# Sums for the projections' quads queued behind weight splits, and attention's moving operands read alternately from two places 2 KB apart

## The chip, the cores and the metric

The kernel runs on one core of one Trainium2 chip. Its time is the device time of one launch in microseconds (us). Five engines work side by side, each with its own queue of instructions: TensorE (PE, with the weight loads shown as PEld), VectorE (DVE), ScalarE (ACT), GpSimd (POOL) and SyncE (SP), which here only issues DMAs. An instruction starts when those ahead of it on its engine have gone and the semaphores that it waits for are set.

## The reference

Two layers over an input x of 256 rows by 2048 columns, all in float32. Layer A projects the normed input to q, k, v and a gate (4096 columns each), does attention in chunks of 64 rows with a bias per relative distance for 32 heads of 128, multiplies by SiLU of the gate and projects back to 2048 columns. Layer B does the same with a shared k and v, a forget gate and a causal mask. Cut to what matters:

```python
h = rms_norm(x, a_norm[layer])                        # layer A
q, k, v, g = jnp.split(h @ a_w_in[layer], 4, axis=-1)
o = chunked_relbias_attention(q, k, v, a_rel_bias[layer])
x = x + (o * jax.nn.silu(g)) @ a_w_out[layer]

h_kv = rms_norm(x, kv_norm)                           # layer B
k_sh, v_sh = jnp.split(h_kv @ kv_w, 2, axis=-1)
cum = cumsum(log_sigmoid(h_kv @ f_w + f_b))
q, g = jnp.split(rms_norm(x, b_norm[0]) @ b_w_in[0], 2, axis=-1)
o = forgetting_attention(q, k_sh, v_sh, cum)
x = x + (o * jax.nn.silu(g)) @ b_w_out[0]
return rms_norm(x, final_norm)
```

## The kernel before, in words

**Products in three parts.** Each float32 operand is split into a high part (rounded to the type fp32r, written by ACT) and a low part (what is left, by a subtraction on DVE). A product is then three fp32r matmuls: high by high, high by low, low by high. `mm3` (L184) does it for the projections, `dot3` (L517 to L519) for attention and for the quads below.

**The stream of weights.** SP loads blocks of 512 KB (256 rows of the weights by 512 columns) into a ring of six raw buffers. `Feed.prepare` splits a block ("hi" on ACT, "lo" on DVE: L247 and L248, in layer B with a gain L242 and L243) into a ring of four hi and lo buffers, three blocks ahead of the block that PE multiplies. One block is 12 matmuls with 512 moving columns. The block lies in SBUF as [128, 2, 2, 256]; `cols` (L70 to L72) makes the moving operand read its 512 columns alternately from the two halves, which are 2 KB apart.

**Groups.** Two heads make a group, 16 groups a layer. A group of layer A is two units of eight blocks (aqk: q and k; avg: v and gate), one of layer B also (bqg: q and gate; bkv: k and v). While PE multiplies one unit, the attention of an earlier group is woven in by a generator (`attention`) that is advanced between blocks. Its steps for one group: DVE transposes q and k in squares of 32 (L487), POOL's queue moves the squares by 16 DMAs (`turned`), ACT and DVE split k and q into "wide" and "q1" (L509, L510), PE makes the scores (s1p, six matmuls of 256 columns, L517 to L519, and s0p, two float32 ones, L541), DVE scales and adds the bias (L548) and takes the maximum (L549), ACT takes the exponential (L551), ACT scales the gate (L562), DVE transposes the lot (`sgY`, L487), 16 DMAs move it (`sgZ`), ACT and DVE split the probabilities into the same "wide" (L509, L510), PE multiplies by v (op, six matmuls of 256 columns and two float32 ones, L575), and DVE multiplies by the gate (L579). A float32 matmul is four passes on PE in the records.

Each "wide" part is a tile of [128, heads, 256], so the 256 moving columns of one head lie next to each other.

**Quads.** After each layer comes the output projection (ao, bo: four units of 512 columns, 16 blocks each). For some pairs of blocks the kernel uses seven products where the plain way has eight (`Quad`): three such quads for ao0 and ao1, five for each later pair. For this, sums of blocks of the attention's output have to be formed: `Quads.open` (L361 to L380) forms five sets. One set is, on DVE, one addition of 128x512 (L371), four of 128x128 (L374 to L377), a copy by ACT (L378) and a subtraction on DVE (L379). The generator is advanced during the blocks ahead of the first quad. A scheduler then places the instructions of each engine by when their inputs are expected, so DVE's instructions for a set stand earlier in its queue than the code has them. `tc.issue_after(x)` keeps the instructions that are made within it behind the instruction x on x's engine. `feed.by_dve` is the latest split that the stream has put on DVE.

The lines are those of the kernel before; in the changed kernel they are up to 13 higher.

## Time and profile before

| what | value |
|---|---|
| time, median of 3 runs | 1755.29 us (1753.59 to 1757.29) |
| the profiled execution's own time | 1757.04 us |
| its span | 1755.3 us |
| PE busy | 1738.7 us, 99% |
| DVE, ACT, POOL busy | 1243.2, 1107.2, 516.6 us |
| DMA | 396.35 MB, mean 226 GB/s |

The span runs from the first instruction of the profile to the last; the 1.74 us by which the time is longer lie around it. A row of the timeline has the start in us, the duration in us, the engine, the line, the operation, the tiles (out <- in), the shape and a count of merged instructions, and in brackets how long the engine sat idle before it and what ended that. Matmuls are pipelined: the duration of one is longer than its distance to the next, so what a matmul costs is read from start to start. The page says also that ends of matmuls are modelled.

### The profile page before, as it was taken

The numbers are of one execution on the slowest core, as the hardware profiler recorded it, in microseconds if no ns is written. First come the engines' busy times: TensorE is split into PE (matmuls) and PEld (weight loads), VectorE is DVE, ScalarE is ACT, GpSimd is POOL, SyncE is SP. The second block draws the span as 40 slices with busy tenths as digits, with TensorE's granted clock in tenths as the row PEclk, the third lists the DMA queues.
The fourth block names the chain that finished last, engine by engine and source line by source line (L and its number), as shares of the span: only waits on it lengthen the run. The fifth ranks groups of instructions, "written<-read, shape, count | busy, mean of one in ns | idle before, by whom it ended". The sixth has DMA issues, their size and how long they took to land.

```text
span 1755.3 us, 25640 instructions
## 1 busy us (share of the span) xinstructions
PE 1738.7 (99%) x8348; PEld 1527.7 (87%) x8348; DVE 1243.2 (71%) x1818; ACT 1107.2 (63%) x2103; POOL 516.6 (29%) x1071
## 2 busy tenths in 40 slices
PE   9999999999999999999999999999999999999997
PEld 7888888888888888888888888888888888888886
DVE  7666666666666686688966777777777777876687
ACT  6555555555555566556657777777777777665454
POOL 2333333333333333202103333333333333333000
PEclk9999999999999999999999999999999999999999
DMA  8776776776777677677767777777767777767654
GB/s 301 241 222 222 227 225 223 226 224 225 224 222 226 224 224 230 202 241 250 245 214 234 226 226 224 224 227 225 224 226 225 225 226 225 245 214 233 218 203 144
DMA packets 143654, 396.35 MB, mean 226 GB/s; under 512 B 31104, under 2 KB 38560, under 8 KB 143392
## 3 DMA queue, kind: packets, MB, share of 16 engines
q1 hardware_dynamic: 107472, 354.25, 62.9%
q0 software_dynamic: 32256, 37.29, 6.5%
q10 hardware_dynamic: 3792, 3.17, 0.6%
q8 instruction: 66, 1.08, 0.3%
q14 instruction: 68, 0.56, 0.1%
HBM read 351.05 MB, written 4.23 MB: 202 GB/s over the span
## 4 chain that ended last, share of the span: by engine, by line
PE 96%; DMA 1%; DVE 1%; ACT 0%; issue 0%; SPq 0%; POOL 0%; DVEq 0%; ACTq 0%
PE bkv_acc L184 19%; PE bqg_acc L184 19%; PE avg_acc L184 18%; PE aqk_acc L184 18%; PE bo_acc L184 8%; PE ao_acc L184 7%; PE op L575 1%; PE s0p L541 1%; PE p L519 0%; PE p L517 0%; PE p L518 0%; PE op L518 0%; PE s1p L518 0%; PE s1p L519 0%; PE s1p L517 0%; PE op L519 0%
## 5 line engine op out<-in xcount | busy, mean ns | idle before, releaser
L490 POOL DMA_DIRECT2D sgZ<-sgY x512 | 251.0, 497 | 193.8 <-DVE sgY L487 90.6
L490 POOL DMA_DIRECT2D turned<-turned x448 | 219.9, 498 | 265.3 <-PE avg_acc L184 94.7
L243 DVE SCALAR_TENSOR_TENSOR bqg_lo<-bqg_raw,gain,bqg_hi 128x512 fp32r<-128x512 f32 x256 | 182.6, 750 | 84.4 <-ACT bqg_hi L242 84.2
L242 ACT ACTIVATE bqg_hi<-bqg_raw,gain 128x512 fp32r<-128x512 f32 x256 | 170.7, 714 | 107.4 <-PE bqg_acc L184 51.8
L248 DVE TENSOR_TENSOR avg_lo<-avg_raw,avg_hi 128x1024 fp32r<-128x1024 f32 x127 | 153.3, 1219 | 109.6 <-ACT avg_hi L247 107.9
L248 DVE TENSOR_TENSOR aqk_lo<-aqk_raw,aqk_hi 128x1024 fp32r<-128x1024 f32 x125 | 152.4, 1219 | 86.8 <-ACT aqk_hi L247 85.4
L247 ACT ACTIVATE avg_hi<-avg_raw 128x1024 fp32r<-128x1024 f32 x127 | 132.4, 1055 | 121.2 <-PE aqk_acc L184 68.6
L243 DVE SCALAR_TENSOR_TENSOR bkv_lo<-bkv_raw,gain,bkv_hi 128x512 fp32r<-128x512 f32 x256 | 181.0, 748 | 38.3 <-ACT bkv_hi L242 35.6
L184 PE MATMUL bqg_acc<-bqg_hi,x1Th 128*128 128x512 f32 x512 | 192.2, 386 | 0.0
L184 PE MATMUL aqk_acc<-aqk_hi,xTh 128*128 128x512 f32 x512 | 190.4, 382 | 1.5 <-ACT aqk_hi L247 1.5
L184 PE MATMUL aqk_acc<-aqk_lo,xTh 128*128 128x512 f32 x512 | 189.1, 380 | 1.2 <-DVE aqk_lo L248 1.2
L184 PE MATMUL avg_acc<-avg_hi,xTh 128*128 128x512 f32 x512 | 190.2, 382 | 0.0
L184 PE MATMUL bqg_acc<-bqg_lo,x1Th 128*128 128x512 f32 x512 | 189.6, 381 | 0.0
L184 PE MATMUL bqg_acc<-bqg_hi,x1Tl 128*128 128x512 f32 x512 | 189.4, 380 | 0.0
L184 PE MATMUL bkv_acc<-bkv_hi,x1Th 128*128 128x512 f32 x512 | 189.1, 380 | 0.0
L247 ACT ACTIVATE aqk_hi<-aqk_raw 128x1024 fp32r<-128x1024 f32 x125 | 131.5, 1052 | 91.2 <-PE aqk_acc L184 43.5
L184 PE MATMUL bkv_acc<-bkv_lo,x1Th 128*128 128x512 f32 x512 | 188.9, 379 | 0.0
L184 PE MATMUL avg_acc<-avg_lo,xTh 128*128 128x512 f32 x512 | 188.9, 379 | 0.0
L184 PE MATMUL avg_acc<-avg_hi,xTl 128*128 128x512 f32 x512 | 188.9, 379 | 0.0
L184 PE MATMUL bkv_acc<-bkv_hi,x1Tl 128*128 128x512 f32 x512 | 188.9, 379 | 0.0
L184 PE MATMUL aqk_acc<-aqk_hi,xTl 128*128 128x512 f32 x512 | 188.9, 379 | 0.0
L242 ACT ACTIVATE bkv_hi<-bkv_raw,gain 128x512 fp32r<-128x512 f32 x256 | 168.7, 712 | 22.9 <-PE bqg_acc L184 16.5
(297 smaller groups left out, 3556.0 us busy)
## 6 DMA issues: line engine op xcount, KB each, us to landing
bqg_raw<-in_b_w_in SPq DMA_DIRECT2D x128, 512.0 KB, 4.3
bkv_raw<-in_kv_w SPq DMA_DIRECT2D x128, 512.0 KB, 4.0
avg_raw<-in_a_w_in SPq DMA_DIRECT2D x127, 512.0 KB, 4.2
aqk_raw<-in_a_w_in SPq DMA_DIRECT2D x125, 512.0 KB, 3.9
ao_raw<-in_a_w_out SPq DMA_DIRECT2D x64, 512.0 KB, 4.4
bo_raw<-in_b_w_out SPq DMA_DIRECT2D x64, 512.0 KB, 4.1
sgZ<-sgY POOLq DMA_DIRECT2D x512, 40.0 KB, 4.0
turned<-turned POOLq DMA_DIRECT2D x448, 32.0 KB, 3.7
```

The costliest lines, as they stand in the source:

```text
L184: pe.matmul(acc[t], x[:, t * P:(t + 1) * P], w, start=t not in begun, stop=last and i == 2)
L242: act.activation(hi[:, :, j], raw[:, :, j], AF.Copy, scale=gk)
L243: dve.scalar_tensor_tensor(lo[:, :, j], raw[:, :, j], gk, r32(hi[:, :, j]), op0=OP.mult, op1=OP.subtract)
L247: self.by_act = act.activation(hi[:, :, j], raw[:, :, j], AF.Copy)
L248: self.by_dve = dve.tensor_sub(lo[:, :, j], raw[:, :, j], r32(hi[:, :, j]))
L490: queues[j].dma_start(out=r32(z)[j * SQ:(j + 1) * SQ, i], in_=y[i * SQ:(i + 1) * SQ, j])
L541: pe.matmul(s0p[:, i], q0[:, i], qkT[:, HG + i, 0], start=True, stop=True)
L575: pe.matmul(op[:, i, P:], v1[:, i * DH:(i + 1) * DH], pT[:, i, NT], start=False, stop=i == HG - 1)
```

## The change

Two parts. In `Quads.open` the work on a set of sums is put within `tc.issue_after(feed.by_dve.ins)`. In `split_pairs` high and low parts become one tile with the two halves t of a head's 256 columns 2 KB apart ("wide") or, for q1, one half; the moving operand then takes a column of each half in turn. The scores and the outputs come out with their columns interleaved, so DVE reads PSUM with a step of two (two instructions for s1p, one per head, where there was one), the float32 matmul of op writes every second column of PSUM, and the forget gate's matmuls (zp, L799 and L800) and their copy go the same way. The tiles in which the start's input lies are named anew.

```diff
--- before.py
+++ after.py
@@ -368,15 +368,16 @@
                 self.sums.append(two[:, b % 2])
                 hi, lo = two[:, b % 2, 0], two[:, b % 2, 1]
                 k = b * KB
-                dve.tensor_add(xs, r32(lhs.hi[k // BIG][:, k % BIG:k % BIG + KB]),
-                               r32(lhs.lo[k // BIG][:, k % BIG:k % BIG + KB]))
-                a11, a21, a12, a22 = (xs[:, j, t * P:(t + 1) * P] for j in range(KB) for t in range(NT))
-                dve.tensor_add(v[:, 0], a21, a22)
-                dve.tensor_sub(v[:, 2], a11, a21)
-                dve.tensor_sub(v[:, 1], v[:, 0], a11)
-                dve.tensor_sub(v[:, 3], a12, v[:, 1])
-                act.activation(hi, v, AF.Copy)
-                dve.tensor_sub(lo, v, r32(hi))
+                with tc.issue_after(feed.by_dve.ins):
+                    dve.tensor_add(xs, r32(lhs.hi[k // BIG][:, k % BIG:k % BIG + KB]),
+                                   r32(lhs.lo[k // BIG][:, k % BIG:k % BIG + KB]))
+                    a11, a21, a12, a22 = (xs[:, j, t * P:(t + 1) * P] for j in range(KB) for t in range(NT))
+                    dve.tensor_add(v[:, 0], a21, a22)
+                    dve.tensor_sub(v[:, 2], a11, a21)
+                    dve.tensor_sub(v[:, 1], v[:, 0], a11)
+                    dve.tensor_sub(v[:, 3], a12, v[:, 1])
+                    act.activation(hi, v, AF.Copy)
+                    dve.tensor_sub(lo, v, r32(hi))
                 yield
 
     def spec(name, w, nk, late=0, kept=0, g0=None):
@@ -499,16 +500,15 @@
 
         out = []
         for srcs, tag in many:
-            nt = srcs[0].shape[1]
-            out.append([att.tile([P, len(srcs), nt * P], F32R, name=f"{tag}{x}", tag=f"{tag}{x}") for x in "hl"])
+            out.append(att.tile([P, srcs[0].shape[1], 2, len(srcs), P], F32R, name=tag, tag=tag))
             if place is not None:
-                feed.behind(out[-1][0][:, :, :1], place)
+                feed.behind(out[-1][:, 0, 0, :, :1], place)
         for k in range(len(many[0][0])):
-            for (srcs, _), (hi, lo) in zip(many, out):
-                h, l = (v[:, k].rearrange("p (t i u) -> p t i u", t=srcs[k].shape[1], u=SQ) for v in (hi, lo))
+            for (srcs, _), both in zip(many, out):
+                h, l = (both[:, :, i, k].rearrange("p t (i u) -> p t i u", u=SQ) for i in range(2))
                 act.activation(h, srcs[k], AF.Copy)
                 dve.tensor_sub(l, srcs[k], r32(h))
-        return out
+        return [[both[:, :, i].rearrange("p t k n -> p k n t") for i in range(2)] for both in out]
 
     def split(srcs, tag, place=None):
         return split_pairs([(srcs, tag)], place)[0]
@@ -536,7 +536,7 @@
         s1p = bank("s1p")[:, :].rearrange("p (i s) -> p i s", i=HG)
         s0p = bank("s0p")[:, :HG * P].rearrange("p (i s) -> p i s", i=HG)
         for i in range(HG):
-            dot3(s1p[:, i], (qh[:, i], ql[:, i]), (kh[:, i], kl[:, i]))
+            dot3(s1p[:, i], (qh[:, i, :, 0], ql[:, i, :, 0]), (kh[:, i], kl[:, i]))
         for i in range(HG):
             pe.matmul(s0p[:, i], q0[:, i], qkT[:, HG + i, 0], start=True, stop=True)
         NB = 1 + NT
@@ -545,7 +545,13 @@
         nm = small.tile([P, NT, HG], F32, name="nm")
         sm = small.tile([P, NT, HG], F32, name="sm")
         for t, sp_, s_, bias in ((1, s1p, sv[:, :, P:], bias1), (0, s0p, sv[:, :, :P], bias0)):
-            dve.scalar_tensor_tensor(s_, sp_, SCALE, bias, op0=OP.mult, op1=OP.add)
+            if t:
+                for i in range(HG):
+                    to, plus = (v[:, i].rearrange("p (t n) -> p t n", t=NT) for v in (s_, bias))
+                    dve.scalar_tensor_tensor(to, sp_[:, i].rearrange("p (n t) -> p t n", t=NT), SCALE, plus,
+                                             op0=OP.mult, op1=OP.add)
+            else:
+                dve.scalar_tensor_tensor(s_, sp_, SCALE, bias, op0=OP.mult, op1=OP.add)
             dve.tensor_reduce(nm[:, t], s_, axis=AX.X, op=OP.max, negate=True)
             for i in range(HG):
                 act.activation(s_[:, i], s_[:, i], AF.Exp, bias=nm[:, t, i:i + 1],
@@ -572,11 +578,12 @@
             cols = slice(i * DH, (i + 1) * DH)
             dot3(op[:, i], (vh[:, cols], vl[:, cols]), (ph[:, i], pl[:, i]), i == 0, False)
         for i in range(HG):
-            pe.matmul(op[:, i, P:], v1[:, i * DH:(i + 1) * DH], pT[:, i, NT], start=False, stop=i == HG - 1)
+            pe.matmul(op[:, i, 1::NT], v1[:, i * DH:(i + 1) * DH], pT[:, i, NT], start=False, stop=i == HG - 1)
         yield
         oT = att.tile([P, HG, S], F32, name="oT", tag="oT")
         for i in range(HG):
-            dve.tensor_mul(*(v[:, i].rearrange("p (t i u) -> p t i u", t=NT, u=SQ) for v in (oT, op)), gT[:, i])
+            dve.tensor_mul(oT[:, i].rearrange("p (t i u) -> p t i u", t=NT, u=SQ),
+                           op[:, i].rearrange("p (i u t) -> p t i u", t=NT, u=SQ), gT[:, i])
         h0 = g * HG
         hi = ocat.hi[h0 // BIG][:, h0 % BIG:h0 % BIG + HG, :]
         lo = ocat.lo[h0 // BIG][:, h0 % BIG:h0 % BIG + HG, :]
@@ -613,10 +620,15 @@
     turned = big_tile([P, 2, NQ, 2 * HG * NT, SQ], F32, name="turned")
     home = [turned[:, i] for i in range(2)]
     xT = Stat("xT", KD)
-    xr, homes = {}, iter(["wideh", "tb", "widel", "oT", "gs", "R", "Y", "Z", "wideh"])
+    xr, homes = {}, iter(["wide", "tb", None, "oT", "gs", "R", "Y", "Z", "wide"])
 
     def load_xT(k0, k1):
-        xr[k0] = att.tile([P, k1 - k0, S], F32, name=f"xr{k0}", tag=next(homes))
+        home_ = next(homes)
+        if home_ is None:
+            xr[k0] = xr["wide"][:, 1]
+        else:
+            both = att.tile([P, 1 + (home_ == "wide"), KB, S], F32, name=f"xr{k0}", tag=home_)
+            xr[k0], xr[home_] = both[:, 0, :k1 - k0], both
         sp.dma_start(out=xr[k0], in_=x_t[:, k0:k1])
 
     def split_xT(k0, k1, by_dve=False):
@@ -796,10 +808,11 @@
         zp = bank("zp")[:2 * H, :S]
         for k in range(KD):
             both = fwp[:, k].rearrange("p a h -> p (a h)")
-            pe.matmul(zp, both, x1T.h(k), start=k == 0, stop=False)
-            pe.matmul(zp, both, x1T.l(k), start=False, stop=k == KD - 1)
+            hi, lo = (v.rearrange("p (t n) -> p n t", t=NT) for v in (x1T.h(k), x1T.l(k)))
+            pe.matmul(zp, both, hi, start=k == 0, stop=False)
+            pe.matmul(zp, both, lo, start=False, stop=k == KD - 1)
         cTs = const.tile([2 * H, S], F32, name="cTs")
-        act.activation(cTs, zp, AF.Copy)
+        act.activation(cTs.rearrange("p (t n) -> p t n", t=NT), zp.rearrange("p (n t) -> p t n", t=NT), AF.Copy)
         zT = cTs[:H]
         yield
         ps = bank("fps")
```

How the instructions move on DVE, at the two places that matter. First in layer B, in the queue of DVE around the scores of one group (bkv_lo: splits of the blocks of bkv14, whose turn on PE comes next; bo_quad and bo_sums: the sums for bo; sg: scores with bias). Before:

```order
L510 TENSOR_TENSOR widel<-turned,wideh 128x256
L510 TENSOR_TENSOR q1l<-turned,q1h 128x128
L371 TENSOR_TENSOR bo_quad<-oBh_8299,oBl_8303 128x512
L243 SCALAR_TENSOR_TENSOR bkv_lo_14789<-bkv_raw_14613,gain,bkv_hi_14788 128x2x256 x2
L379 TENSOR_TENSOR bo_sums_16048<-bo_quad,bo_sums_16048 128x512
L374 TENSOR_TENSOR bo_quad<-bo_quad 128x128
L375 TENSOR_TENSOR bo_quad<-bo_quad 128x128
L376 TENSOR_TENSOR bo_quad<-bo_quad 128x128
L243 SCALAR_TENSOR_TENSOR bkv_lo_14826<-bkv_raw_14667,gain,bkv_hi_14825 128x2x256 x2
L377 TENSOR_TENSOR bo_quad<-bo_quad 128x128
L379 TENSOR_TENSOR bo_sums_16048<-bo_quad,bo_sums_16048 128x512
L548 SCALAR_TENSOR_TENSOR sg<-s1p,cb 128x2x256
```

and with the change:

```order
L510 TENSOR_TENSOR wide<-turned,wide 128x2x128
L510 TENSOR_TENSOR q_14751<-turned,q_14751 128x128
L243 SCALAR_TENSOR_TENSOR bkv_lo_14730<-bkv_raw_14555,gain,bkv_hi_14729 128x2x256 x2
L243 SCALAR_TENSOR_TENSOR bkv_lo_14765<-bkv_raw_14609,gain,bkv_hi_14764 128x2x256 x2
L243 SCALAR_TENSOR_TENSOR bkv_lo_14807<-bkv_raw_14635,gain,bkv_hi_14806 128x2x256
L551 SCALAR_TENSOR_TENSOR sg<-s1p,cb 128x256 x2
L554 SCALAR_TENSOR_TENSOR sg<-s0p,d_14590 128x2x128
```

The sums are gone from this place; in the changed kernel they stand between the splits bo1_lo7 and bo2_lo5, in the output projection itself. The scores of this group have now the same neighbours as in the groups before it.

Second, DVE ahead of the first quad of ao (wide<-sgZ: the split of the last group's probabilities; quad_lo: the split of the quad's first block). Before:

```order
L510 TENSOR_TENSOR widel<-sgZ,wideh 128x256 x2
L248 TENSOR_TENSOR ao_lo_6993<-ao_raw_6850,ao_hi_6992 128x1024
L248 TENSOR_TENSOR ao_lo_7019<-ao_raw_6877,ao_hi_7018 128x1024
L288 TENSOR_TENSOR ao_quad<-ao_raw_6904,ao_raw_6902 128x2x256
L295 TENSOR_TENSOR quad_lo_7051<-ao_raw_6902,quad_hi_7050 128x1024
L579 TENSOR_TENSOR oT<-op,sgZ 128x256
```

and with the change:

```order
L510 TENSOR_TENSOR wide<-sgZ,wide 128x2x128 x2
L248 TENSOR_TENSOR ao_lo_6960<-ao_raw_6818,ao_hi_6959 128x1024
L380 TENSOR_TENSOR ao_sums_6886<-ao_quad,ao_sums_6886 128x512
L372 TENSOR_TENSOR ao_quad<-oAh_185,oAl_189 128x512
L375 TENSOR_TENSOR ao_quad<-ao_quad 128x128
L376 TENSOR_TENSOR ao_quad<-ao_quad 128x128
L377 TENSOR_TENSOR ao_quad<-ao_quad 128x128
L248 TENSOR_TENSOR ao_lo_6986<-ao_raw_6845,ao_hi_6985 128x1024
L378 TENSOR_TENSOR ao_quad<-ao_quad 128x128
L288 TENSOR_TENSOR ao_quad<-ao_raw_6872,ao_raw_6870 128x2x256
L295 TENSOR_TENSOR quad_lo_7018<-ao_raw_6870,quad_hi_7017 128x1024
L380 TENSOR_TENSOR ao_sums_6977<-ao_quad,ao_sums_6977 128x512
```

In the kernel before, the five sets for ao stand among the splits of layer A's last three groups. Now all five stand in the queue between the split ao0_lo8 and the end of the first quad's first split; the rows show the end of the fourth set and the fifth. The additions of a set go around the splits that the stream has given later. PE's own order is the same in both kernels.

On SP the loads of two residual tiles (`xin`) in ao move back by six and eight places; on POOL, at one place (the 16 DMAs of `sgZ` that follow these scores), the masking of the next group's `cb` (L866) stands behind the DMAs, as it does in the groups before, and no longer ahead of them; ACT's copies L378 move with the sums.

## The prediction

> **What bounds the kernel now.** I read the profile's page first: the busy shares, the row of granted clocks, the chain that ended last.
>
> ```profile
> PE 1738.7 (99%) x8348; PEld 1527.7 (87%) x8348; DVE 1243.2 (71%) x1818; ACT 1107.2 (63%) x2103; POOL 516.6 (29%) x1071
> PEclk9999999999999999999999999999999999999999
> PE 96%; DMA 1%; DVE 1%; ACT 0%; issue 0%; SPq 0%; POOL 0%; DVEq 0%; ACTq 0%
> ```
>
> PE is busy for 1738.7 of 1755.3 us at nearly the full clock, and the chain is PE for 96%. So only two things can move the end: what a matmul costs from its start to the next one's start, and the few places where PE waits. Everything on DVE, ACT or a queue counts only through such a wait.
>
> Next I read PE's timeline inside an attention step of layer A (projection, scores, projection), then the weight loads at the same place, then the outputs of the last group of layer A.
>
> ```profile
> 399.70 0.38 PE L184 MATMUL avg_acc<-avg_hi,xTh 128*128 128x512 f32 x1
> ...
> 402.93 0.28 PE L517 MATMUL s1p<-wideh,q1h 128*128 128x256 f32 x1
> 403.06 0.28 PE L518 MATMUL s1p<-widel,q1h 128*128 128x256 f32 x1
> ...
> 403.65 0.61 PE L541 MATMUL s0p<-turned,q 128*128 128x128 f32 x4
> ```
>
> ```profile
> 403.54 0.53 PEld L541 LDWEIGHTS s0p<-turned,q 128*128 128x128 f32 x4
> 403.99 0.30 PEld L184 LDWEIGHTS aqk_acc<-aqk_hi,xTh 128*128 128x128 f32 x2
> ```
>
> ```profile
> 736.41 0.28 PE L517 MATMUL op<-wideh,vh 128*128 128x256 f32 x1
> ...
> 737.13 0.61 PE L575 MATMUL op<-sgZ,v 128*128 128x128 f32 x4
> ```
>
> Between 399.70 and 402.93 lie 15 projection matmuls of 512 columns: 3.23 / 15 = 215 ns each, 0.42 ns a column. They read alternately from two halves. The scores read 256 columns that lie in a row: five of them from 403.06 to 403.65, 118 ns each; the six of op take 0.72 / 6 = 120. Half of 215 is 107.7, so these short matmuls carry 11 ns that the long ones don't. There are two suspects. One is the form of reading, which the change alters. The other is the weight load, of which a matmul needs one: four loads start between 403.54 and 403.99, 112 ns each, with almost nothing else to wait for (their matmuls have 128 columns, some 54 ns). A load of 112 explains no more than about 112 of the 119. The third witness is the forget gate, whose matmuls also read 256 columns in a row but load only 64 columns of weights:
>
> ```profile
> L799 PE MATMUL zp<-x1Th,fwp x16: 276/276/282, 897.4 to 900.8; 128*64 128x256 f32 x16
> L800 PE MATMUL zp<-x1Tl,fwp x16: 276/276/279, 897.5 to 900.9; 128*64 128x256 f32 x16
> ```
>
> 32 starts from 897.4 to 900.9 are 31 gaps of 113 ns: still 5 over the half, with half the load. So a load seems to disturb a reading in a row, by about 5 ns for 64 columns and 11 for 128, and the alternating form at 512 columns, under the same 128-column loads, shows none of it.
>
> **Part one, the alternating reading.** How many matmuls it touches is in the groups by shape; each product of the scores and of op has 64, six such rows in all, 384 matmuls; the float32 ones stand below them.
>
> ```profile
> L517 PE MATMUL s1p<-wideh,q1h 128*128 128x256 f32 x64 | 18.0, 282 | 0.0
> L575 PE MATMUL op<-sgZ,v 128*128 128x128 f32 x128 | 19.7, 276 | 0.0
> ```
>
> The best case is 107.7 ns each: 384 x 11.3 = 4.3 us. If loads bind at 112, it is 384 x 7 = 2.7 us. At nothing gained it is 0. I take 110, between the two rows that it is nearest to: 384 x 9 = **3.4 us less**. The 32 zp matmuls can gain 32 x 5 = 0.2 us at most; their halves are 512 bytes apart, not 2 KB; I take 0.1.
>
> A rule speaks against this. The Trainium skill, page "SBUF — State Buffer", section "Specifications (TRN2)", says that SBUF has lines of 16 bytes, that two hits a line are needed for full bandwidth and that each cross to a new line is penalised; reading by turns from two halves crosses at every column. The rows of the projections disagree: 215 ns for 512 such columns. By the rule the term above would be a loss, by the rows it is a gain, and the rows have it.
>
> DVE pays for it: one L548 over two heads (0.60 us from its start to the next, 1512.98 to 1513.58 in the rows of DVE below) becomes two of the size of the s0p one (0.33, 1513.58 to 1513.91), 0.06 us more a group. It also reads PSUM with a step of two there and in L579. No row shows what that costs: at best nothing, at worst, as an assumption, twice the time, which is 0.66 for the scores and the same for the two L579. These lie in the chain from the scores to op, whose slack is worked out below as 2.7 us, so I take 0. Without that cover it would be up to 1.3 us a group. The float32 part of op writes every second column of PSUM. Its passes are held at about 112 ns by their loads while 128 columns need 54, so a write at up to twice the time is hidden: 0, and the case beyond it is a rival.
>
> **Part two, the sums of bo.** The largest wait of PE in layer B is one op, late in the layer; here beside the op of the group before:
>
> ```profile
> 1493.30 0.28 PE L517 MATMUL op<-wideh,vh 128*128 128x256 f32 x1
> ...
> 1536.84 0.38 PE L184 MATMUL bqg_acc<-bqg_hi,x1Tl 128*128 128x512 f32 x1
> 1538.58 0.39 PE L517 MATMUL op<-wideh,vh 128*128 128x256 f32 x1 [1.36 <-ACT wideh L509]
> 1539.04 0.39 PE L518 MATMUL op<-widel,vh 128*128 128x256 f32 x1
> ...
> 1540.24 0.74 PE L184 MATMUL bqg_acc<-bqg_hi,x1Th 128*128 128x512 f32 x1
> ...
> 1543.74 0.38 PE L184 MATMUL bqg_acc<-bqg_hi,x1Tl 128*128 128x512 f32 x1
> ```
>
> The op could have started at 1536.84 + 0.22 = 1537.06. It lost 1.52 us to the first wait, 0.34 to the second, and then the eight matmuls from 1540.24 to 1543.74 took 3.50 us instead of 8 x 0.215 = 1.72: they ran slower after the pause, 1.78 more. Together 3.6 us. Why was it late? A group lasts 1537.06 - 1493.30 = 43.76 us, and the steps of ACT and DVE stand against that:
>
> ```profile
> 1459.77 0.42 ACT L509 ACTIVATE wideh<-turned 128x256 fp32r<-128x256 f32 x1 [2.06 <-DMA turned<-turned]
> 1490.15 0.72 ACT L509 ACTIVATE wideh<-sgZ 128x256 fp32r<-128x256 f32 x2
> 1505.28 0.42 ACT L509 ACTIVATE wideh<-turned 128x256 fp32r<-128x256 f32 x1 [3.82 <-DMA turned<-turned]
> 1538.11 0.72 ACT L509 ACTIVATE wideh<-sgZ 128x256 fp32r<-128x256 f32 x2 [4.24 <-DMA turned<-turned]
> ```
>
> ```profile
> 1465.28 0.68 DVE L548 SCALAR_TENSOR_TENSOR sg<-s1p,cb 128x512 f32<-128x512 f32 x1
> ...
> 1506.81 0.68 DVE L371 TENSOR_TENSOR bo_quad<-oBh,oBl 128x512 f32<-128x512 f32 x1
> ...
> 1509.45 0.29 DVE L374 TENSOR_TENSOR bo_quad<-bo_quad 128x128 f32<-128x128 f32 x1
> 1509.66 0.28 DVE L375 TENSOR_TENSOR bo_quad<-bo_quad 128x128 f32<-128x128 f32 x1
> ...
> 1512.37 0.69 DVE L379 TENSOR_TENSOR bo_sums<-bo_quad,bo_sums 128x512 fp32r<-128x512 f32 x1
> 1512.98 0.68 DVE L548 SCALAR_TENSOR_TENSOR sg<-s1p,cb 128x512 f32<-128x512 f32 x1
> 1513.58 0.41 DVE L548 SCALAR_TENSOR_TENSOR sg<-s0p,d 128x256 f32<-128x256 f32 x1
> 1513.91 1.00 DVE L549 TENSOR_REDUCE nm<-sg 128x2 f32<-128x512 f32 x2
> ```
>
> The first split is 1505.28 - 1459.77 - 43.76 = 1.75 us late: the DMAs of `turned` landed late. The scores' bias is 1512.98 - 1465.28 - 43.76 = 3.94 late: another 2.2, and between 1506.81 and 1512.98 DVE did sums. The last split is 4.2 late, PE waited 1.5, so the slack of the chain is 2.7. Either lateness alone (1.75 or about 2.2 to 2.5) fits into 2.7; both do not. The change takes the sums away there, so the 3.6 us go, in the executions that have them. One whose DMAs are in time has no wait already. The three runs before spread over 3.7 us, and 1757.04 - 3.6 = 1753.4 is about the fastest of them (1753.59): I take the profiled execution as one with the wait and the fastest as one without.
>
> The sums now run during bo itself, where DVE is idle for 26 of 65 us while PE never is:
>
> ```profile
> 1585.00:1650.00 65.00, 65.00 (x316) 57.38 (x315) 39.21 (x48) 33.58 (x55) 12.62 (x26) 1.00 0.69 220
> ```
>
> A set is 0.61 + 4 x 0.21 (1509.45 to 1509.66) + 0.61 (1512.37 to 1512.98) = 2.1 us and is given every two blocks, 24 x 0.215 = 5.2 us of PE, in which the two splits need another 2.3: hidden.
>
> **Part two, the sums of ao.** Here there is no such room. Five sets, 10.5 us, now stand ahead of or between the splits of the first quad. The rows of DVE and PE there:
>
> ```profile
> 732.18 0.69 DVE L289 TENSOR_TENSOR ao_quad<-ao_raw 128x512 f32<-128x512 f32 x1 [3.62 <-DMA ao_raw<-in_a_w_out]
> 732.79 1.22 DVE L248 TENSOR_TENSOR ao_lo<-ao_raw,ao_hi 128x1024 fp32r<-128x1024 f32 x1
> ...
> 742.94 1.23 DVE L295 TENSOR_TENSOR quad_lo<-ao_quad,quad_hi 128x1024 fp32r<-128x1024 f32 x1 [0.25 <-ACT quad_hi L294]
> 744.08 0.69 DVE L295 TENSOR_TENSOR quad_lo<-ao_raw,quad_hi 128x512 fp32r<-128x512 f32 x1
> ```
>
> ```profile
> 746.86 0.38 PE L518 MATMUL p<-quad_lo,ao_sums 128*128 128x512 f32 x1
> ...
> 748.80 0.38 PE L518 MATMUL ao_acc<-quad_lo,oAh 128*128 128x512 f32 x1
> ```
>
> L289 waits for its load, so three sets and a piece pass before 732.2 in DVE's idle time. Behind it, in the new order up to the second split of the quad, stand five splits at 1.14 (742.94 to 744.08; 5.7), two L380, one L372, L288, L297 and L298 at 0.61 to 0.7 (as from 732.18 to 732.79; 3.8), the small additions (eight at 0.2: 1.6), the splits of wide (0.7) and two L579 (0.7): 12.5 us from 732.8, so 745.3, and 745.8 with a wait for ACT's high part. PE wants it at 746.86. The fourth split follows after an oAl (0.6), a half split (0.6) and itself (1.14): 748.2 against 748.80. Both are in time, by 0.5 to 1 us. I take 0.1 us, with 1.5 as the other end (a load 2 us later). The moved loads of `xin` are wanted blocks later and the masking on POOL a group later: 0.
>
> **The sum**, against the profiled execution: 1757.04 - 3.4 - 0.1 - 3.6 + 0.1 = **1750.0 us**; from the fastest run 1753.59 - 3.4 = 1750.2, which I forecast. Against the median of 1755.29 this is 5.1 us, 0.3%.
>
> **Rivals.** *The reading changes nothing* (the 119 ns are the load's doing after all; the rows for it are the 112 of the float32 loads, against it the 215 of the projections): only the wait goes, 1750.0 + 3.5 = 1753.5. *The wait stays*, because the late DMAs alone suffice (the sums' own part, 2.2 of 3.9, speaks against it): 1750.0 + 3.6 = 1753.6, less in executions with DMAs in time. *The first quad of ao waits*: a load of L289 that lands 2 us later makes PE pause by about 1.5 and run slow after it as at 1540 (1.8): 1753.3. *Slower: the step of two in PSUM.* L575's 128 passes write every second column; if such a column costs over two columns' time (112 / 54), it decides; at four it is 4 x 54 - 112 = 104 ns a pass, 13.3 us: 1763. At three it is 6.4 us, 1756.4. No row of the trace has such a write. The Trainium skill, page "PSUM — Partial Sum Buffer", section "Specifications (TRN2)", says that any non-contiguous pattern slows matmuls significantly, without a figure; no run here shows it yet.
>
> **Chances.** The forecast 0.5, the reading changes nothing 0.2, the wait stays 0.1, the first quad waits 0.1, the step in PSUM 0.1. A measurement here tells about 0.2% (3.5 us) from no change. The forecast lies 5 us below, nearly all of it beyond that (0.47); of the three rivals around 1753.5, whose terms may combine with part of the gain, 0.1 does; the PSUM rival is slower for 0.07 and something unseen for 0.02. So faster 0.57, same 0.34, slower 0.09. The range takes the terms' ends on the fast side (4.3 and some spread of runs: 1748.2) and reaches over the rivals at 1753.5 to 1755.8; the forecast's own is 1748.6 to 1751.8.
>
> **What would show it.** Right: starts of the scores' matmuls 108 to 112 ns apart; the op near 1534 without an idle time ahead of it; the second quad_lo of ao done ahead of the third product of the quad. Wrong: scores still at 118 (first rival), a wait ahead of one late op (second), an idle time with the releaser L295 or a quad_hi near 745 (third), passes of L575 over 112 ns apart (last). A mean of L548 and L579 per element far above 0.33 us per 256 says that a step of two costs DVE time.

## The result, and the profile after

| | before | changed |
|---|---|---|
| time, median of 17 runs each | 1753.91 us (1752.32 to 1757.41) | 1751.45 us (1749.94 to 1753.24) |
| ratio, 95% interval | | 0.9983 (0.9976 to 0.9991) |
| span of the profiled execution | 1755.3 us | 1749.7 us |

The change gains 2.5 us in the median (0.14%) and 0.17% by the ratio. The ratios, here and below, are not quotients of the medians; they stand nearer to those of the means (here 1751.56 and 1754.49). The gain is clear of no change by the interval, but below the 0.2% that I had set as the bound of what can be told. The time is 1.25 us above the forecast of 1750.2. The two profiled spans differ by 5.6 us, more than twice as much as the medians: the profiled execution of before (1757.04) was one of its slowest.

The page of the changed kernel, busy shares and the chain that ended last:

```profile
PE 1734.4 (99%) x8348; PEld 1522.3 (87%) x8348; DVE 1245.2 (71%) x1850; ACT 1108.1 (63%) x2103; POOL 516.9 (30%) x1071
PE 93%; DVE 3%; DMA 2%; issue 1%; ACT 1%; SPq 0%; POOL 0%; DVEq 0%
```

PE's share of the chain fell from 96 to 93%, and DVE and DMA have some: somewhere PE waits that did not before. First the reading, PE's timeline at the scores that the prediction showed, the forget gate's matmuls by their first and last starts, and the groups by shape of DVE's readings of PSUM and of op's float32 passes on PE:

```profile
402.28 0.27 PE L517 MATMUL s1p<-wide,q 128*128 128x256 f32 x1
402.39 0.28 PE L518 MATMUL s1p<-wide,q 128*128 128x256 f32 x1
...
402.95 0.61 PE L541 MATMUL s0p<-turned,q 128*128 128x128 f32 x4
```

```profile
L812 PE MATMUL zp<-x1Th,fwp x16: 272/272/273, 897.1 to 900.4; 128*64 128x256 f32 x16
L813 PE MATMUL zp<-x1Tl,fwp x16: 273/273/273, 897.2 to 900.5; 128*64 128x256 f32 x16
```

```profile
L551 DVE SCALAR_TENSOR_TENSOR sg<-s1p,cb 128x256 f32<-128x256 f32 x32 | 12.0, 417 | 1.0 <-PE s1p L519 1.0
L585 DVE TENSOR_TENSOR oT<-op,sgZ 128x256 f32<-128x256 f32 x64 | 24.0, 416 | 0.0
```

```profile
L581 PE MATMUL op<-sgZ,v 128*128 128x128 f32 x128 | 19.6, 276 | 0.0
```

Six scores' matmuls take 0.67 us, 112 ns each, where they took 118 to 120: the pace of the weight loads (112). The forget gate's, with half the load, take 3.4 / 31 = 110 ns (113 before). DVE reads PSUM with a step of two in 416 ns per 256 columns (415 before), and the float32 passes, which write every second column, keep their mean of 276 ns: the step of two costs nothing that shows. Since ends of matmuls are modelled, the four passes are better read from the start of the first to the start of the next matmul: 0.36 us in the changed kernel (735.68 to 736.04), 0.37 before (737.13 to 737.50).

At the op of layer B that waited before, PE's timeline shows no pause; but at the first quad of ao there is one. There, for the changed kernel, PE, then DVE, then SP's queue:

```profile
1535.59 0.27 PE L517 MATMUL op<-wide,vh 128*128 128x256 f32 x1
1535.70 0.28 PE L518 MATMUL op<-wide,vh 128*128 128x256 f32 x1
```

```profile
748.43 0.38 PE L184 MATMUL ao_acc<-ao_hi,oAh 128*128 128x512 f32 x1
750.32 0.48 PE L184 MATMUL ao_acc<-ao_lo,oAh 128*128 128x512 f32 x1 [1.52 <-DVE ao_lo L248]
```

```profile
744.21 0.68 DVE L295 TENSOR_TENSOR quad_lo<-ao_raw,quad_hi 128x512 fp32r<-128x512 f32 x1
745.18 1.23 DVE L295 TENSOR_TENSOR quad_lo<-ao_raw,quad_hi 128x1024 fp32r<-128x1024 f32 x1 [0.29 <-ACT quad_hi L294]
748.44 0.69 DVE L289 TENSOR_TENSOR ao_quad<-ao_raw 128x512 f32<-128x512 f32 x1 [2.03 <-DMA ao_raw<-in_a_w_out]
749.05 3.49 DVE L248 TENSOR_TENSOR ao_lo<-ao_raw,ao_hi 128x1024 fp32r<-128x1024 f32 x3
```

```profile
744.92 0.33 SPq L206 DMA_DIRECT2D ao_raw<-in_a_w_out  x1
```

Read backwards: PE loses 750.32 - 748.43 - 0.22 = 1.67 us for the low part of ao1's block 4. Its split (749.05) stands on DVE behind L289, the preparation of the second quad, which waits for a block to land. SP issues that block's load at 744.92, when the third split of the first quad (744.21 + 0.68 = 744.89) has read its raw buffer empty. In the kernel before, that split was at 744.08 and the load at 744.79, almost the same; but PE wanted the low part only at 750.10, 1.45 us later than now (748.65), and did not wait:

```profile
749.88 0.38 PE L184 MATMUL ao_acc<-ao_hi,oAh 128*128 128x512 f32 x1
750.10 0.38 PE L184 MATMUL ao_acc<-ao_lo,oAh 128*128 128x512 f32 x1
```

### The profile page after: what moved, and what is told of

It is laid out like the page before. It is cut to its first block, busy times and chain, and to the rows that moved or that the text cites. A ratio compares the mean times of both kernels' runs of the same rounds, so it can differ in the third digit from the quotient of the medians.

```text
span 1749.7 us, 25685 instructions
## 1 busy us (share of the span) xinstructions
PE 1734.4 (99%) x8348; PEld 1522.3 (87%) x8348; DVE 1245.2 (71%) x1850; ACT 1108.1 (63%) x2103; POOL 516.9 (30%) x1071
## 4 chain that ended last, share of the span: by engine, by line
PE 93%; DVE 3%; DMA 2%; issue 1%; ACT 1%; SPq 0%; POOL 0%; DVEq 0%
PE bkv_acc L184 19%; PE bqg_acc L184 19%; PE avg_acc L184 19%; PE aqk_acc L184 19%; PE bo_acc L184 7%; PE ao_acc L184 5%; PE op L581 1%; PE s0p L541 1%; DMA bo_raw<-in_b_w_out 1%; DVE quad_lo L295 1%; DMA ao_raw<-in_a_w_out 0%; DVE ao_lo L248 0%; DMA xr<-in_x_t 0%; PE op L518 0%; PE s1p L519 0%
```

## The experiments

The timed kernels are compared with runs of the kernel before on the same chip, whose median differed from chip to chip (1753.4 to 1755.6), so ratios are compared across them.

**One part at a time.** Four kernels, side by side. The alternating reading alone, with the sums as before:

```diff
-                with tc.issue_after(feed.by_dve.ins):     # in the changed kernel's Quads.open
+                # as before
```

> The kernel before with the alternating reading alone; the sums stay where the scheduler put them. Theory: the reading is worth what the profile after shows, 384 matmuls at 112 instead of 119 ns, 2.9 us in every execution; the wait of about 3.6 us at 1537 stays possible here, as before, so the median falls by 2.5 to 3.0 us against before. At the first quad of ao PE comes 1.4 us sooner but DVE is free of sums, so no wait over 0.4 us there. Rival one (the gain of the change is the removed wait, the reading is worth nothing): no change in the time. Rival two (PE's earlier arrival alone runs into the load of the second quad): a wait of about 1.5 us ahead of the split of ao1's block 4, and a gain of only 1.5 us.

The changed kernel with only bo's sums queued, and the kernel before with both sums queued, and with bo's alone:

```diff
-                with tc.issue_after(feed.by_dve.ins):
+                with tc.issue_after(feed.by_dve.ins) if self.name == "bo" else ExitStack():
```

> The changed kernel with only the sums of bo queued behind the splits; those of ao stand as before. Theory: the wait of 1.7 us at 748 in the profile after comes from ao's sums, which hold up the quad's third split on DVE and with it the release of the raw buffer into which the second quad's block is loaded; without them it goes: no wait over 0.4 us at the first quad, and 1.0 to 1.7 us faster than the changed kernel, 3.3 to 4.2 us faster than before. Rival two (the load alone, once PE is early): the wait stays at about 1.5 us and the time is that of the changed kernel, 2.5 us below before.

> The kernel before with both sets of sums queued behind the splits, and the reading as before. Theory: the op at 1537 does not wait (3.6 us in the executions that have this wait, which by the medians are the minority), the first quad of ao waits little, since PE arrives 1.4 us later there than in the changed kernel: 0.2 to 0.5 us. The median falls by 0 to 0.7 us. Rival one (the removed wait is all of the gain): 2.4 us below before.

> The kernel before with only the sums of bo queued. Theory: as the kernel with both, without the 0.2 to 0.5 us at ao: 0.2 to 1.0 us below before in the median, with the slowest executions (1757) gone. Rival (the wait at 1537 comes from late DMAs whatever the sums do): the median and the slowest stay as before.

| kernel | reading | sums queued | median, 11 runs | slowest | ratio to before (33 runs, 1753.43, slowest 1757.81) |
|---|---|---|---|---|---|
| read_only | by turns | none | 1750.55 | 1754.92 | 0.9987 (0.9978 to 0.9996) |
| read_bo | by turns | bo | 1750.13 | 1750.88 | 0.9980 (0.9971 to 0.9988) |
| sums_only | in a row | ao and bo | 1754.22 | 1756.23 | 1.0006 (0.9997 to 1.0015) |
| bo_only | in a row | bo | 1753.21 | 1753.66 | 0.9996 (0.9988 to 1.0005) |

The reading is worth 2.9 us by the medians (1753.43 - 1750.55), as 384 matmuls at 112 for 119 ns give, and 3.1 between the two kernels with bo's sums queued (1753.21 - 1750.13). Queueing bo's sums hardly moves the median (0.2 us without the reading, 0.4 with it), but it takes away the long executions: of the 33 of before 14 lie above 1753.7 and of the 11 with the reading alone 4 above 1752.0; with bo's sums alone queued none. In the means, which long executions move, the term is 0.8 and 1.2 us. Queueing ao's sums too costs 1.0 us (1754.22 against 1753.21), so that sums_only rose by 0.8 in the median where a fall of 0 to 0.7 was expected. In the profile of the kernel with both sums and the old reading, the same place of PE's timeline has a wait of about half the size; its DVE had the third split of the quad at 744.64:

```profile
749.38 0.38 PE L184 MATMUL ao_acc<-ao_hi,oAh 128*128 128x512 f32 x1
750.48 0.48 PE L184 MATMUL ao_acc<-ao_lo,oAh 128*128 128x512 f32 x1 [0.72 <-DVE ao_lo L248]
```

That is 0.88 us, above the 0.2 to 0.5 expected. With ao's sums left alone and the reading changed (read_bo), DVE, SP and PE there read:

```profile
741.99 0.68 DVE L295 TENSOR_TENSOR quad_lo<-ao_raw,quad_hi 128x512 fp32r<-128x512 f32 x1
744.97 1.23 DVE L295 TENSOR_TENSOR quad_lo<-ao_raw,quad_hi 128x1024 fp32r<-128x1024 f32 x1 [2.30 <-ACT quad_hi L294]
746.12 0.68 DVE L289 TENSOR_TENSOR ao_quad<-ao_raw 128x512 f32<-128x512 f32 x1
```

```profile
742.70 0.33 SPq L206 DMA_DIRECT2D ao_raw<-in_a_w_out  x1
```

```profile
748.21 0.38 PE L184 MATMUL ao_acc<-ao_hi,oAh 128*128 128x512 f32 x1
748.43 0.38 PE L184 MATMUL ao_acc<-ao_lo,oAh 128*128 128x512 f32 x1
```

The third split is 2.2 us sooner than in the changed kernel, the load follows it by the same 0.03 us, L289 finds its block there, and PE goes on without a pause. So the wait is the sums', by way of a raw buffer that they keep full; PE's earlier arrival alone (the rival of read_only and read_bo) does not make it: in the profile of read_only PE has no pause there either. This kernel has a spread of 1.3 us and a median 3.3 us below before on its chip; the changed one's was 2.5 below before on another, so 0.8 us apart. The two were not run beside each other, and the intervals of their ratios overlap; what shows it faster is the wait that is gone.

**Fewer sums ahead of the first quad.** Two of ao's five sets, which only ao2 and ao3 need, are formed between the first quads:

```diff
-(ao_quads.open(oA, QUADS), [3, 1, 1, 2, 2])
+(ao_quads.open(oA, QUADS), [3, 1, 1, 10, 4])
```

> The changed kernel with two of the five sets of ao, those that only the later quads (of ao2 and ao3) need, advanced between the first three quads instead of ahead of them; three sets stay queued behind splits ahead of the first quad. Theory: the wait at 748 is DVE's backlog of sums; with 4 us less of it the quad's third split is done at 742 to 743 us instead of 744.2, and the wait shrinks below 0.4 us; but DVE has sums between the quads now, where up to 1 us of new waits may come. Time between the kernel with ao's sums left alone (1750.1) and the changed one (1751.4). Rival (queueing behind splits in itself, by moving the loads of xin in SP's queue): the wait at 748 stays at 1.7 us.

10 runs gave 1750.45 us (1749.08 to 1750.96) against 1755.55 of before on that chip, 0.9970 (0.9961 to 0.9980). There is no wait at 748; DVE's third split is at 742.29. By itself this does not settle the rival: the edit also moved the load of `xin` that SP issues just ahead of the late block in the changed kernel (738.55) to 763.46, behind these quads. The rows of the other runs do. In the changed kernel that load has landed after 4.7 us, before the block's load is issued at 744.92; the block's load then takes 3.4 us to land, against 3.2 in the kernel before (744.79) and 3.1 in read_bo (742.70), where no `xin` stands ahead of it. And DVE has no idle time from 730.48 until the third split has ended. So the backlog of sums is the cause. All four profiles at the usual pace with five sets queued ahead of this quad have the wait, 0.67 to 1.67 us (the changed kernel, sums_only and the kernels row_apart and near_512 below); of the nine others at that pace none has it.

**What in the reading counts.** Three forms, one run each. In the first the halves lie 2 KB apart but are read one after the other; in the second the 256 columns lie next to each other and are read with a step of two, the even ones first; in the third the halves are read by turns, 512 bytes apart.

```diff
-        return [[both[:, :, i].rearrange("p t k n -> p k n t") ...     # changed kernel: by turns, 2 KB
+        return [[both[:, :, i].rearrange("p t k n -> p k t n") ...     # one half after the other
+        ... both[:, i] of [P, 2, k, t, P], "p k (t n) -> p k (n s)", read "p k s n"    # step of two
+        return [[both[:, i].rearrange("p k t n -> p k n t") ...        # by turns, 512 bytes
```

> The changed kernel, with the two halves of a head's 256 columns 2 KB apart as there, but read one half after the other (128 columns in a row each) for the scores and op; the columns then come out in their order and DVE is as in the kernel before. Theory: what counts is that neighbouring columns are taken from different places; in a row the scores' and op's matmuls are back at 118 to 119 ns from start to start. Rival (the new place of the tile, or the distance of the halves, did it): 112 ns as in the changed kernel.

> The changed kernel with the 256 columns of a head next to each other, as before the change, but read with a step of two columns: the even ones first, then the odd ones. Theory A (a reading in a row collides with the weight load because it takes neighbouring columns at once; any step frees it): 112 ns. Theory B (what frees it is the turn between two places far apart): 118 to 119 ns, as before. By a rule of 16-byte lines (two hits a line) a step of two columns of 4 bytes still has two hits, the change's turn between halves one: it would have this form at least as fast as the changed kernel's.

> The changed kernel with the two halves of a head's 256 columns 512 bytes apart instead of 2 KB, read in turn as there. Theory: the turn counts, not the distance (the forget gate's halves are 512 bytes apart and its matmuls fell to 109 ns): 112 ns for the scores and op. Rival (2 KB is needed under a weight load of 128 columns): 115 ns or more.

PE's timeline at the same scores, the three in this order:

```profile
402.38 0.28 PE L517 MATMUL s1p<-wide,q 128*128 128x256 f32 x1
...
403.10 0.61 PE L541 MATMUL s0p<-turned,q 128*128 128x128 f32 x4
```

```profile
412.92 0.41 PE L518 MATMUL s1p<-wide,q 128*128 128x256 f32 x1
...
414.06 0.62 PE L541 MATMUL s0p<-turned,q 128*128 128x128 f32 x4
```

```profile
401.50 0.27 PE L517 MATMUL s1p<-wide,q 128*128 128x256 f32 x1
...
402.17 0.61 PE L541 MATMUL s0p<-turned,q 128*128 128x128 f32 x4
```

One half after the other: 0.72 / 6 = 120 ns, as before the change, so the new place of the tile does nothing; the run took 1753.24 us. With a step of two: five in 1.14 us, 228 ns, twice as long, and the whole run took 1795.68 us; theory A falls, and theory B, which had 118 to 119 for this form, missed too. By turns at 512 bytes: 0.67 / 6 = 112 ns, as at 2 KB, and 1750.58 us. Taking neighbouring columns from two places is what counts, and not every way of leaving the row is good.

**The wait at 1537.** My reading was that two latenesses together exceed a slack of 2.7 us. I tried to make the sums heavier, in the kernel before:

```diff
-                dve.tensor_add(xs, ...)
+                for _ in range(3 if self.name == "bo" else 1):
+                    dve.tensor_add(xs, ...)
```

> The kernel before with the first addition of each set of bo's sums done three times (the same result), 1.2 us more of DVE time a set, at the places where the scheduler puts them. Theory: the wait at 1537 is the sums' lateness against a slack of 2.7 us; with about 2.4 us more ahead of the score's bias and the transposition it comes in nearly every execution, 2 us or more and then the slow clock: the median rises by 2 to 5 us over the kernel before. Rival (late DMAs cause it): the median stays within 0.7 us of before.

10 runs: 1753.98 us against 1755.55, ratio 0.9995 (0.9986 to 1.0005). The expectation did not come in, but the run could not test it: the scheduler put most of the additional work behind the scores or into DVE's wait for `turned`, and from ACT's split of `turned` to the scores' bias DVE took 7.40 us (1503.08 to 1510.48), no more than the 7.70 of before (1505.28 to 1512.98). The op lost 0.72 us in the profile, as sums of that size may. So I put the delay into the chain itself, in the kernel read_bo, for this group alone:

```diff
+            if t and ocat.name == "oB" and g == 13:
+                for _ in range(3):      # 7 in the second
+                    dve.scalar_tensor_tensor(s_, s_, 1.0, s_, op0=OP.mult, op1=OP.max)
             dve.tensor_reduce(nm[:, t], s_, axis=AX.X, op=OP.max, negate=True)
```

> The faster kernel (alternating reading, only bo's sums queued behind splits) with three more instructions of 128x512 (the maximum of the scores with themselves, 0.6 us each) on DVE behind the scaled scores of the one group of layer B whose op waited in the profile before, so that its chain is 1.8 us later and nothing else changes. Theory: the slack of the chain is 2.7 us, so that op does not wait (under 0.3 us). Rival (the slack is far smaller, and 1.8 us of lateness does it alone, as the late DMAs of the profile before were 1.75): a wait of 1 us or more.

> The same with seven such instructions, 4.2 us, the lateness of the profile before. Theory: the op waits about 1.5 us, loses 0.3 us more at the next matmul, and the eight or so matmuls behind it run at half speed: 3 to 4 us in all over the faster kernel, some 1753.5 us. Rival (lateness on DVE is taken up elsewhere, the wait had another cause): no wait over 0.3 us, 1750.1 us.

The transposition on DVE of the group before and of this one without the delay (read_bo), then that of this group and its op in the run with three, then with seven:

```profile
1469.60 1.51 DVE L488 STREAM_TRANSPOSE sgY<-sg 128x1280 f32<-128x1280 f32 x1 [0.28 <-ACT sg L568]
...
1515.01 1.51 DVE L488 STREAM_TRANSPOSE sgY<-sg 128x1280 f32<-128x1280 f32 x1 [0.28 <-ACT sg L568]
```

```profile
1517.03 1.51 DVE L489 STREAM_TRANSPOSE sgY<-sg 128x1280 f32<-128x1280 f32 x1 [0.41 <-ACT sg L572]
```

```profile
1533.78 0.38 PE L185 MATMUL bqg_acc<-bqg_hi,x1Tl 128*128 128x512 f32 x1
1534.77 0.38 PE L518 MATMUL op<-wide,vh 128*128 128x256 f32 x1 [0.61 <-ACT wide L510]
1535.23 0.38 PE L519 MATMUL op<-wide,vh 128*128 128x256 f32 x1
```

```profile
1521.96 1.51 DVE L489 STREAM_TRANSPOSE sgY<-sg 128x1280 f32<-128x1280 f32 x1 [0.41 <-ACT sg L572]
```

```profile
1534.46 0.38 PE L185 MATMUL bqg_acc<-bqg_hi,x1Tl 128*128 128x512 f32 x1
1540.23 0.58 PE L518 MATMUL op<-wide,vh 128*128 128x256 f32 x1 [5.39 <-ACT wide L510]
...
1542.63 0.77 PE L185 MATMUL bqg_acc<-bqg_hi,x1Th 128*128 128x512 f32 x1
...
1545.68 0.38 PE L185 MATMUL bqg_acc<-bqg_lo,x1Th 128*128 128x512 f32 x1
```

Both expectations missed in size. Two us of delay made a wait of 0.77 us (and 0.35 at the next matmul) where none was expected; that run took 1751.85 us. In the second the seven instructions were spread between weight splits, so the delay was 6.3 us (1521.96 - 1515.01, less 0.68 that PE itself was later) and the wait 5.55; it took 1758.85 us. The slack in this group is then 1.25 and 0.75 us, not 2.7. The difference lies in the group: read_bo's transposition is itself 1515.01 - 1469.60 - 43.68 = 1.7 us late against that of the group before, at 1469.60, with no sums near, since `turned` lands late. With these 1.7 counted in, the slack is 3.0 and 2.5, on both sides of the 2.7. The mechanism, lateness on DVE that reaches PE beyond a slack of this size, holds; that it can be had without any sum shows that sums are not the only source.

**Where `turned` is late from.** In the windows of the changed kernel, with DMA's share and GB/s in the last columns, and in the list of DMA issues, stands what shares the queue:

```profile
1480.00:1491.00 11.00, 11.00 (x52) 9.63 (x52) 7.73 (x12) 7.39 (x14) 3.54 (x8) 1.00 0.73 220
1491.00:1503.00 12.00, 12.00 (x62) 10.63 (x62) 6.88 (x12) 5.76 (x13) 6.07 (x13) 1.00 0.93 322
```

```profile
gfin<-in_final_norm SPq DMA_DIRECT2D x1, 1024.0 KB, 7.1
```

The load of the final norm's gain, 1 MB at 1495.4 us (1496.7 before), meets the DMAs of `turned` of exactly this group, in the profile of each kernel but the last. So the lateness is built in and not an accident of one execution, as I had taken it; only its size differs. In bo_only, where the sums are gone and this load is not, ACT's split of `turned` is 2.0 us late and DVE's transposition is not (each row beside that of the group before; a group lasts 43.76 us):

```profile
1457.18 0.42 ACT L510 ACTIVATE wideh<-turned 128x256 fp32r<-128x256 f32 x1 [0.23 <-DMA turned<-turned]
...
1502.94 0.42 ACT L510 ACTIVATE wideh<-turned 128x256 fp32r<-128x256 f32 x1 [2.24 <-DMA turned<-turned]
```

```profile
1471.68 1.51 DVE L488 STREAM_TRANSPOSE sgY<-sg 128x1280 f32<-128x1280 f32 x1
...
1515.49 1.51 DVE L488 STREAM_TRANSPOSE sgY<-sg 128x1280 f32<-128x1280 f32 x1
```

In read_bo the split is 3.9 us late and the transposition 1.7. What DVE makes of it stands in the split of this group and the scores' bias on DVE, in read_bo (no sums between them) and in read_only (sums as before):

```profile
1502.36 0.42 ACT L509 ACTIVATE wide<-turned 128x256 fp32r<-128x256 f32 x1 [3.90 <-DMA turned<-turned]
1507.76 0.75 DVE L551 SCALAR_TENSOR_TENSOR sg<-s1p,cb 128x256 f32<-128x256 f32 x2
```

```profile
1500.86 0.42 ACT L508 ACTIVATE wide<-turned 128x256 fp32r<-128x256 f32 x1 [2.81 <-DMA turned<-turned]
1508.57 0.75 DVE L550 SCALAR_TENSOR_TENSOR sg<-s1p,cb 128x256 f32<-128x256 f32 x2
```

From the one to the other DVE's queue takes 5.40 us without the sums (5.39 to 5.40 in every profile that has them elsewhere and this load here) and 7.71 with them (7.70 before the change). So the sums are worth 2.3 us here, and of the 3.94 by which the bias was late before, 1.6 are left for `turned`. In the profiles without sums or added delay at this place the transposition came up to 2.4 us late (late_two) and PE did not wait for op; with sums and the load it came 3.2 us late (read_only: 0.15 lost at op's second matmul), 3.4 (bo_heavy: 0.7) and 4.2 (before: 1.5 and 0.34). So this load alone, as late as it was in these profiles, does not make the wait. For the sums alone the rows give an estimate only: a split in time stands 5.7 us ahead of the scores on PE (bo_only, the group before: 1457.18 and 1462.89), and the bias follows the start of the scores by 1.63; so with 7.7 us of queue the bias would be 0.4 us late.

The last run moved this load, in the kernel before:

```diff
-    sp.dma_start(out=gfin, in_=...)                 # ahead of bo
+        if u == 0 and left == 5:                    # in bo_begun
+            with tc.issue_after(feed.by_sp.ins):    # by_sp: the latest load of a weight block
+                sp.dma_start(out=gfin, in_=...)
```

> The kernel before with one load moved: the 1 MB of the final norm's gain (gfin), which SP issues at 1496.7 us beside the DMAs of `turned` of the group whose op waited, is issued during bo0 instead, about 120 us later. Sums and reading as before the change. Theory: two latenesses make the wait at 1537, this load's (1.75 us on `turned`, in every kernel looked at) and that of bo's sums (2.2 us); with the load away the sums alone stay within the slack of 2.7 us: `turned` is in time, the group's transposition on DVE is no more than 2.5 us late, no wait at its op, and the slowest executions (1754.5 and more) go: median 0.2 to 1.0 us below before. Rival (the sums alone suffice): the wait and the spread stay.

12 runs: 1753.38 us (1752.60 to 1755.05) against 1754.78 (1752.38 to 1760.03), 0.9988 (0.9978 to 0.9997). The median fell by 1.4 us, more than the 0.2 to 1.0 expected, and the long executions went but for one of 1755.05; `turned` and the transposition were in time. So the load is what makes `turned` late, for in the other profiles it is late with the sums there and without them. But the run doesn't separate the two causes of the wait: with the load gone from there the scheduler also moved bo's sums, to 1608 to 1626 us. What sums do without this load is not shown by any run, only by the estimate above.

## Why the prediction was right or wrong

**The bound** was read rightly: everything gained or lost is in the pace of matmuls or in a few waits of PE.

**The alternating reading** went as forecast in kind and a little smaller in size: 112 ns for the 110 taken, 2.9 us for 3.4, the lower of the two bounds given (2.7). The pace is that of "if loads bind at 112"; that it is the loads which bind is read from this agreement and from the 110 ns of the forget gate beside loads of 64 columns, not from a run that changes the load alone. The forget gate gave 0.1 as taken. The rule of 16-byte lines (the Trainium skill, page "SBUF — State Buffer", section "Specifications (TRN2)"), which I had set aside by the rows of the projections, does not order the forms tried: a turn between two places, one hit a line, is the fastest (112 ns) and a step of two, with two hits, the slowest (228 ns). The costs put at nothing, DVE's and PE's step of two in PSUM, were nothing here (416 ns for 415, 276 for 276), so the slower rival falls, for passes that a weight load holds at 112 ns.

**The sums of bo**: the removed wait was real, and the profiled execution had it (3.6 us), but the step that failed is "against the profiled execution" as a measure for the median: the median of three runs given (1755.29) stood 1.4 us above that of 17 (1753.91), and the term is worth 0.2 to 0.4 us in a median (0.8 to 1.2 in a mean), since most executions of before hardly wait there. I had said so ("one whose DMAs are in time has no wait already") and made the forecast from the fastest run, which is why the time came out within 1.3 us. That the fastest of three lay near the median of 17 was luck. How seldom before waits is inferred from its times; the two other profiles with sums and load at this place lost 0.15 and 0.7 us. The 5.1 us of difference were still too many, and with them the 0.57 given to a gain beyond 0.2%. The lateness of `turned` was wrong in kind: it is late in all 13 profiles that have the load of 1 MB there. The 1.75 us that I read for it were taken against a group whose own DMAs had come late (the 2.06 of its row); against a split 5.7 us ahead of the scores it was 3.6. What differs from one profile to the next is whether the lateness of the transposition, 0 to 4.2 us, crosses a slack of 2.5 to 3 us.

**The sums of ao** is the step that failed by its result: "Both are in time, by 0.5 to 1 us. I take 0.1 us". Both splits were in time: the second split of the quad began at 742.48 and the fourth at 745.18, sooner than I had worked out. I stopped there. Next in the queue stood L289 of the second quad, and its load hangs on the third split, which the sums hold up, while part one lets PE arrive 1.45 us sooner. Measured: 1.67 us in the profile, 0.8 by the medians of the changed kernel and read_bo against before on their chips, 1.0 with the old reading. The third rival named the first quad and a late load of the first L289; the place was the first quad's end, and the load the second's. The end of 1.5 given for this term covers the medians; the one profile lies a little beyond it.

**The sum again**, with these sizes, from the median of 17 (the forget gate's 0.1 lies in the measured 2.9): 1753.91 - 2.9 - 0.3 + 1.0 = 1751.7, against 1751.45.

## What to carry to other kernels

A wait that one profiled execution shows is worth its size times how often it comes: look at the spread of the runs before adding it to a gain. When work is queued ahead of a hand-over, follow not only the consumers of that hand-over but what its buffers release: here the load that waited for a raw buffer to be read came late one quad further on. And when two edits are put together, add up where the engines then stand against each other. Here PE came 1.45 us sooner to the place where the sums made the load late; but that this made the wait dearer is not shown: the profiles with the new reading have 1.67 and 0.76 us (near_512), those with the old pace 0.88 and 0.67 (row_apart), and by the medians the sums of ao cost 0.8 and 1.0.

## What the runs showed of the hardware that I had not expected

A matmul of 256 fp32r columns beside a load of 128 weight columns takes 118 to 120 ns when it reads its columns in a row, 112 when it takes them by turns from two places 512 bytes or 2 KB apart, and 228 when it reads every second column of a row. With a load of 64 columns the first two are 113 and 110. A pause of PE of 0.8 us (late_18) or 1.67 us (the changed kernel) left the pace of the matmuls behind it as it was; one of 5.5 us (late_42) was followed by 5.4 us at half the pace, from 1540.2 to 1545.7, and the 1.5 us of the kernel before by 3.5 us that began 1.7 us after it, at a granted clock of 0.51. Length alone does not decide it: in late_two two pauses of 1.18 and 0.90 us, 0.1 apart at 80 us, left the granted clock at 1.00. Trainium2's clock gate, in the Trainium skill, page "TensorE: Matmul & The Clock Gate", section "What's actually happening", watches activity in a free-running window of about 3.4 us and gives the slow state after an idle window of that length. The 5.5 us of late_42 agree with this; the 1.5 us of before do not, for they are shorter than such a window and the slow stretch came all the same. Whether it counts where in a window a pause falls is not shown: no run here varied the place alone.
